# Hybrid SSD and attention block on one core: attention's product of probabilities and values as three float32r products

## The chip, the core and the metric

The kernel runs on one core of a Trainium2 chip. Its time is the device time of one execution in microseconds (us), the median of several runs. TensorE (PE) multiplies, VectorE (DVE) and ScalarE (ACT) do element-wise work, GpSimd (POOL) a little of it, and SyncE (SP) issues most transfers. Each engine works through its own list of instructions in order and waits on semaphores for the others.

## The reference, cut to what matters

One decoder block for 1024 tokens of width 1024. An SSD branch and a differential-attention branch read the same normed input; gates merge them, and a convolutional FFN follows. The attention branch, cut to its core:

```
q, k = partial_rope(...)                      # 16 half heads of 64
v = v.reshape(bsz, seq, 8, 128)               # 8 heads
for i in range(8):                            # query blocks of 128, causal
    s = einsum(q[block i], k[:q1]) * scale    # q1 = 128 * (i + 1)
    p = softmax(where(mask, s, -inf))
    attn = p[first of pair] - lam * p[second of pair]
    o[block i] = einsum(attn, v[:q1])
o = rms_norm(o, subln_w) * (1 - lam_init)
```

All is float32. The kernel reaches float32's accuracy in most of its matrix products with three float32r products, of a rounded high part and the remaining low part of each operand: high by high, high by low, low by high.

## The kernel before, in words

TensorE's lists of work are written out by hand (`manual_schedule` keeps the program's order on the engines that it names; in attention these are PE, DVE, ACT and POOL, while the order of SP's transfers there is the scheduler's). The stages are: the normed input with its first products; the projections of SSD and gates; the SSD stage, during which v is projected as filler; q and k and the output projection of SSD; attention, with the rest of q and k and the attention gate as filler; attention's output projection, the merge and `w_out`; the FFN's up and down products.

**v.** `v_stream` (L1018 on) makes v in 16 tiles of 128 tokens by 512 channels, each of 8 x 3 float32r products into a `wa` bank of PSUM (L1028 to L1030). ACT copies a tile into one half of the slot `vev`, and it is written to `vd` in memory as float32 (L1044). The generator is advanced by `fill(n)`, a few products at a time, between the SSD steps.

**Attention** goes over 64 items, 8 heads of 8 query blocks. For item t the list reads: `scores(t+1)`, in which the transposes of item t stand behind the score products (`behind`) and ahead of the mask and the maximum; `fill`; for i >= 4 the second half of the transposes; `probs(t+1)`, that is exponentials on ACT, then reciprocal, coefficient and the combination of both probabilities on DVE; `values(t)`; `fill`; the second half of values. A call of `fill` gives three products of 512 columns from `dense_stream`. 248 such calls are shared out over the items, and 20 are kept for each end.

`transposes(t, k0)` (L1496) turns up to four 128x128 blocks of the combined probabilities into the one `wb` bank (L1502), and ACT copies them to `aT` as float32 (L1503). `values` (L1508) multiplies each block with v's block of the same keys, one float32 product each (L1515), into a `wc` bank that gathers four query blocks. The mask is added at L1465 or L1475, the maximum taken at L1466 or L1476, the exponentials at L1478, L1486 and L1489, and the combination is L1492 to L1494. `load_heads` (L1426) fetches a head's v from `vd` into `vt`, two slots in turn, and `norm_o` and `out_o` norm and transpose the result.

`Slots` hands out 43 buffers of 4 KB per partition. `run_bg` and `later` keep a queue of small pieces for ACT and DVE, for instance the splits of the dense weights into high and low parts (L1381, L1384).

Of the kernel before, what the change touches and what calls it, by code (L numbers as in the profile page):

```python
# [11 lines left out]
F32 = mybir.dt.float32  # L12
F32R = mybir.dt.float32r
AF = mybir.ActivationFunctionType
ALU = mybir.AluOpType
AX = mybir.AxisListType

P = 128
D = 1024
S = 1024  # L20
HALF = 512
# [41 lines left out]
def kernel(ctx: ExitStack, tc: tile.TileContext, a: dict, out: bass.AP, dbg=None):  # L63
# [351 lines left out]
    sel = const("sel_r", [P, NH], F32R)  # L415

    zd = [dp.tile([P, D], F32, tag=f"zd{i}", name=f"zd{i}") for i in range(8)]
    vd = [dp.tile([P, D], F32, tag=f"vd{i}", name=f"vd{i}") for i in range(8)]
    yd = [dp.tile([P, D], F32, tag=f"yd{i}", name=f"yd{i}") for i in range(8)]
    gsd = [dp.tile([P, S], F32, tag=f"gsd{j}", name=f"gsd{j}") for j in range(8)]  # L420
    gad = [dp.tile([P, S], F32, tag=f"gad{j}", name=f"gad{j}") for j in range(8)]
# [533 lines left out]
    pairs_of_banks = ExitStack()  # L955
    pmm = pairs_of_banks.enter_context(tc.tile_pool(name="pmm2", bufs=1, space=bass.MemoryType.PSUM))
    BT, CT = [xbcT[8], xbcT[9]], [xbcT[10], xbcT[11]]
    vev = SL.get("vev", F32, (P, 2, HALF))

    SL.put(hi_t)  # L960

# [56 lines left out]
    def v_stream():  # L1018
        for vh in range(2):
            for i in range(8):  # L1020
                ps = ps_wa(f"v{vh}_{i}")
                half, q = divmod(i, 4)
                tsl = slice(q * P, (q + 1) * P)
                for k in range(KD):
                    need(("wv", vh, k // 2))
                    wh, wl = wv[vh, k // 2][0][:, k % 2, :], wv[vh, k // 2][1][:, k % 2, :]
                    xh_, xl_ = hT[k][half][:, 0, tsl], hT[k][half][:, 1, tsl]
                    T.matmul(ps, xh_, wh, start=(k == 0), stop=False)  # L1028
                    T.matmul(ps, xh_, wl, start=False, stop=False)  # L1029
                    T.matmul(ps, xl_, wh, start=False, stop=(k == KD - 1))  # L1030
                    if k % 2 == 0 and ((vh == 0 and i == 7 and k > 0) or (vh == 1 and i == 0 and k < 4)):
                        if v_low:
                            v_low.pop()()
                            if k == 4 and vh == 0:
                                v_raw.append(fetch_v(1, 3))
                        if v_raw:
                            v_low.append(split_v(1, (k // 2 - 1) % 4, v_raw.pop(0)))
                    if k < KD - 1:
                        yield
                if vh == 0 and i == 5:  # L1040
                    v_raw.extend(fetch_v(1, kp) for kp in range(3))
                e = vev[:, i % 2, :]
                A.copy(e, ps)
                SP.dma_start(vd[i][:, vh * HALF : (vh + 1) * HALF], e)  # L1044
                yield

    v_raw, v_low = [], []
# [202 lines left out]
            for r in range(2):  # L1250
                SP.dma_start(dst[64 * r : 64 * r + 64, :].bitcast(F32), src[m])

    SL.put(vev)
    yT = [[None] * 2 for _ in range(KD)]

    n_turn = 0
# [81 lines left out]
        SL.put(*yT[k])  # L1338


    vt = [SL.get(f"vt{i}", F32, (P, 8, P)) for i in range(2)]
    for t, n in ((qst, "qst"), (kst, "kst"), (klo, "klo")):
        t.append([SL.get(f"{n}1_{s}", F32R) for s in range(2)])
    thl = [[SL.get(f"tq{n}{i}", F32R) for n in ("hi", "lo")] for i in range(2)]
    pt_ = [[SL.get(f"p{b}_{s}") for s in range(2)] for b in range(2)]
    aTs = [SL.get(f"aT{i}", F32, (P, 2, 4, P)) for i in range(1)]
    osb = SL.get("osb", F32, (P, 2, 4, P))
    gev = SL.get("gev", F32, (P, 2, HALF))

    ssum = const("ssum", [P, 2, 2])  # L1350
    nmx = const("nmx", [P, 2, 2])
    rsm = const("rsm", [P, 2, 4, 2])
# [6 lines left out]
    blocks = [(kind, b) for b in (3, 4, 5) for kind in ("w_q", "w_k")] + [("ga", 0)]  # L1359
    blocks += [(kind, b) for b in (6, 7) for kind in ("w_q", "w_k")] + [("ga", g) for g in range(1, 8)]  # L1360
    emitted = {"scores": 0, "values": 0}
    raws, splits = {}, {}
    finished.clear()

# [32 lines left out]
    def dense_stream():  # L1397
        fetch(0)
        fetch(1)
        split_later(0)  # L1400
        for n, (kind, j) in enumerate(blocks):
            fetch(n + 2)
            need(("w", n))
            split_later(n + 1)
            w = splits.pop(n)
            for half in range(2):
                ps = ps_wa(f"{kind}p{j}_{half}")
                for k in range(KD):
                    xh_, xl_ = hT[k][half][:, 0, :], hT[k][half][:, 1, :]
                    T.matmul(ps, w[0][:, k, :], xh_, start=(k == 0), stop=False)  # L1410
                    T.matmul(ps, w[0][:, k, :], xl_, start=False, stop=False)
                    T.matmul(ps, w[1][:, k, :], xh_, start=False, stop=(k == KD - 1))
                    if k < KD - 1:
                        yield
                hsl = slice(half * HALF, (half + 1) * HALF)
                if kind == "ga":
                    A.activation(gev[:, half, :], ps, AF.Tanh, scale=0.5)
                    SP.dma_start(gad[j][:, hsl], gev[:, half, :])
                else:
                    hi, lo = thl[n % 2]  # L1420
                    A.activation(hi[:, hsl], ps, AF.Copy, scale=qscale[kind])
                    low_part(kind, j, half, ps, hi, lo)
                yield

    def load_heads(j):
        b = j % 2  # L1426
        last = 2 + ((j + 1) * 96 - 1) // P
        if last > 2:
            need(("low", "w_k", last, 1))
        assert emitted["scores"] >= 8 * (j - 1) and emitted["values"] >= 8 * (j - 1)  # L1430
        if j > 0:
            for s in range(2):
                load_qk(2 * j + s, qst[b][s], kst[b][s], klo[b][s])
        for kt in range(8):
            SP.dma_start(vt[b][:, kt, :], vd[kt][:, j * P : (j + 1) * P])

    stream = dense_stream()

# [57 lines left out]
    def transposes(t, k0):  # L1496
        j, i = items[t]
        nk = min(4, i + 1 - k0)
        ptr = ps_wb(f"at{j}_{i}_{k0}")
        at = aTs[0][:, (k0 // 4 + i) % 2]  # L1500
        for k in range(nk):
            T.transpose(ptr[:, k * P : (k + 1) * P], pt_[i % 2][0][:, (k0 + k) * P : (k0 + k + 1) * P], ident)  # L1502
        A.copy(at[:, :nk].rearrange("p k q -> p (k q)"), ptr[:, : nk * P])  # L1503
        return at, nk

    po_of = {}
# [1 line left out]
    def values(t, k0, at, nk):  # L1508
        j, i = items[t]
        grp, qi = divmod(i, 4)  # L1510
        if qi == 0 and k0 == 0:
            po_of[j, grp] = ps_wc(f"o{j}_{grp}").rearrange("p (q d) -> p q d", d=P)
        for k in range(nk):
            kt = k0 + k
            T.matmul(po_of[j, grp][:, qi, :], at[:, k, :], vt[j % 2][:, kt, :], start=(kt == 0), stop=(kt == i))  # L1515

    ob, oe = osb[:, 0], osb[:, 1].rearrange("p q d -> p (q d)")

# [73 lines left out]
    with tc.manual_schedule(engines={EN.PE, EN.DVE, EN.Activation, EN.Pool}):  # L1592
# [6 lines left out]
        for t, (j, i) in enumerate(items):  # L1599
            quota = (j * sum(share) + sum(share[: i + 1])) * nfill // (8 * sum(share)) - done  # L1600
            done += quota
            quota += 2 if t == len(items) - 2 else 0
            f1 = quota // 2
            nxt = t + 1 < len(items)
            x = {}

            def first_turn():
                x[0] = transposes(t, 0)

            if nxt:  # L1610
                sc = scores(t + 1, first_turn)
            else:
                first_turn()
            fill(f1)
            f2 = (quota - f1 + 1) // 2
            if i >= 4:
                x[4] = transposes(t, 4)
            if nxt:
                probs(t + 1, sc, 2)
            run_bg(1)  # L1620
            values(t, 0, *x[0])
            fill(f2)
            if i % 4 == 2 and pend is not None:
                out_o(*pend)
            if i >= 4:
                values(t, 4, *x[4])
            fill(quota - f1 - f2)
            run_bg(1)
            emitted["values"] += 1
            if t == 55:  # L1630
                SL.put(*thl[0], *thl[1], *qst[0], *kst[0], *klo[0], vt[0])
                stg = [SL.get(f"stg{i}", F32, (P, 2, HALF)) for i in range(2)]
                for _ in range(4):
                    att_in()
            elif t > 56:
                for _ in range(2 if i % 2 else 1):
                    if n_att < 10:
                        att_split()
            if j < 7 and i == (4 if j == 0 else 3):
                load_heads(j + 1)  # L1640
            if i % 4 == 3:
                norm_o(j, i // 4)
                pend = (j, i // 4)
            elif i % 4 == 2:
                pend = None
        SL.put(*pt_[0], *qst[1], *kst[1], *klo[1], *pt_[1], vt[1], *aTs)
        for n in range(NLAST - 2):
            if n == 11:
                out_o(*pend)
            if n == 1:  # L1650
                fetch_ao(0)
            fill(1)
            run_bg(1)
            if n % 2 == 1 and n < 9:
                att_split()
            if n == 13:
                split_ao(0)
        run_bg(len(bg))
        assert n_att == len(parts)
        SL.put(osb, gev, *stg)  # L1660
        for k in range(KD):
            SL.put(*hT[k])

# [757 lines left out]
```

## Time and profile before

| | |
|---|---|
| median of 3 runs | 1842.9 us (1842.53 to 1843.33) |
| profiled execution: span, first to last instruction | 5463.1 us |
| profiled execution: another time of its own | none is given beside the span |
| PE, PEld busy | 5447.4 us, 3303.6 us |
| DVE, ACT, POOL busy | 1312.2 us, 898.9 us, 139.0 us |
| DMA moved | 326.22 MB |
| granted TensorE clock in the records | 1.00 |

PE stands for products, PEld for loads of their stationary operand, which overlap products. The profiled execution took 2.96 times as long as the timed ones. Counts, order and shapes of its rows are those of the timed runs, and so is what an engine does; how far the durations on TensorE carry over is a matter for the prediction. In the trace, a float32 product stands as two records, a float32r product and a transpose as one.

### The profile page before, as it was taken

How to read it: one execution, taken by the hardware profiler on the slowest of the kernel's cores; microseconds unless marked ns; L12 is line 12 of the kernel's file. 1: busy time of each engine (PE TensorE's matmuls, PEld its weight loads, DVE VectorE, ACT ScalarE, POOL GpSimd, SP SyncE). 2: the span in 40 equal slices, each digit the busy share in tenths (PEclk: the TensorE clock that was granted, in tenths of full speed). 3: DMA queues.
4: the chain of work that ended last, by engine and by line, in shares of the span. 5: the costliest groups of instructions: out<-in, count | busy, mean ns of one | idle time of the engine just before them, and what ended most of it. 6: DMA issues, size and time to landing. Idle time of an engine off the chain costs nothing.

```text
span 5463.1 us, 24362 instructions
## 1 busy us (share of the span) xinstructions
PE 5447.4 (100%) x8922; PEld 3303.6 (60%) x8922; DVE 1312.2 (24%) x1984; ACT 898.9 (16%) x1744; POOL 139.0 (3%) x128
## 2 busy tenths in 40 slices
PE   9999999999999999999999999999999999999999
PEld 4555557766665555566677776556555555555555
DVE  4122222222221200022222231212333333332211
ACT  3111110011111100011122221102212111121210
POOL 0000000001110000000000000000000000000000
DMA  4021012212111212121122112210011111123221
GB/s 165 31 77 46 29 35 72 70 64 100 64 67 46 54 35 81 35 52 47 48 72 69 56 47 95 81 46 31 31 44 39 44 35 41 40 71 116 87 63 60
DMA packets 131368, 326.22 MB, mean 60 GB/s; under 512 B 14881, under 2 KB 39089, under 8 KB 131250
## 3 DMA queue, kind: packets, MB, share of 16 engines
q1 hardware_dynamic: 130290, 321.53, 18.2%
q0 software_dynamic: 960, 3.15, 0.2%
q8 instruction: 70, 1.15, 0.1%
q14 instruction: 48, 0.39, 0.0%
HBM read 229.45 MB, written 95.17 MB: 59 GB/s over the span
## 4 chain that ended last, share of the span: by engine, by line
PE 100%; issue 0%; ACT 0%; POOL 0%; DVE 0%; DMA 0%; DVEq 0%; POOLq 0%; ACTq 0%
PE upx L1822 4%; PE upx L1823 4%; PE upx L1821 4%; PE o L1515 4%; PE v L1028 2%; PE z L116 2%; PE v L1029 2%; PE z L118 2%; PE z L117 2%; PE xx L534 2%; PE so L117 2%; PE so L118 2%; PE xx L532 2%; PE upy L1821 2%; PE upy L1822 2%; PE upy L1823 2%
## 5 line engine op out<-in xcount | busy, mean ns | idle before, releaser
L1515 PEld LDWEIGHTS o<-vt,aT 128*128 128x128 f32 x576 | 201.1, 415 | 39.5 <-issue 33.8
L1821 PE MATMUL upx<-t,wu_t 128*128 128x512 f32 x264 | 218.9, 829 | 0.0
L1823 PE MATMUL upx<-t,wu_t 128*128 128x512 f32 x264 | 218.7, 828 | 0.0
L1822 PE MATMUL upx<-t,wu_t 128*128 128x512 f32 x264 | 218.7, 828 | 0.0
L1515 PE MATMUL o<-vt,aT 128*128 128x128 f32 x576 | 214.2, 578 | 0.0
L1456 PE MATMUL sc<-kst,qst 128*128 128x512 f32 (+2 forms) x192 | 141.7, 742 | 0.0
L1457 PE MATMUL sc<-klo,qst 128*128 128x512 f32 (+2 forms) x192 | 141.4, 746 | 0.0
L118 PE MATMUL so<-yT,w_ssd_o_lo 128*128 128x512 f32 x128 | 140.8, 1100 | 0.0
L117 PE MATMUL so<-yT,w_ssd_o_hi 128*128 128x512 f32 x128 | 140.8, 1100 | 0.0
L116 PE MATMUL so<-yT,w_ssd_o_hi 128*128 128x512 f32 x128 | 139.3, 1088 | 0.0
L1503 ACT COPY aT<-at 128x512 f32<-128x512 f32 (+2 forms) x96 | 45.9, 479 | 562.2 <-PE at L1502 562.2
L1822 PEld LDWEIGHTS upx<-t,wu_t 128*128 128x128 f32 x264 | 93.5, 354 | 63.8 <-issue 63.8
L1821 PEld LDWEIGHTS upx<-t,wu_t 128*128 128x128 f32 x264 | 93.4, 354 | 63.7 <-issue 62.7
L1823 PEld LDWEIGHTS upx<-t,wu_t 128*128 128x128 f32 x264 | 92.3, 350 | 63.8 <-issue 63.8
L1114 PEld LDWEIGHTS py<-xd,M 128*128 128x128 f32 x256 | 107.1, 596 | 34.8 <-issue 34.8
L1028 PE MATMUL v<-wv_hi,hT 128*128 128x512 f32 x96 | 121.5, 1266 | 0.0
L116 PE MATMUL z<-wz_hi,hT 128*128 128x346 f32 (+1 forms) x144 | 121.1, 841 | 0.0
L118 PE MATMUL z<-wz_hi,hT 128*128 128x346 f32 (+1 forms) x144 | 119.7, 832 | 0.0
L117 PE MATMUL z<-wz_lo,hT 128*128 128x346 f32 (+1 forms) x144 | 119.1, 827 | 0.0
L1502 PE MATMUL at<-ident,p 128*128 128x128 f32 x288 | 117.1, 576 | 0.0
L2184 PE MATMUL dx<-wdt_hi,g_hi 128*128 128x512 f32 x132 | 109.5, 830 | 0.0
L2186 PE MATMUL dx<-wdt_hi,g_lo 128*128 128x512 f32 x132 | 109.2, 827 | 0.0
(553 smaller groups left out, 10212.8 us busy)
## 6 DMA issues: line engine op xcount, KB each, us to landing
adas<-in_w_ada SPq DMA_DIRECT2D x32, 512.0 KB, 3.9
wdr<-in_w_down SPq DMA_DIRECT2D x22, 512.0 KB, 5.5
wtd<-wds SPq DMA_DIRECT2D x22, 512.0 KB, 2.9
wuf<-in_w_up SPq DMA_DIRECT2D x22, 512.0 KB, 3.5
gld_s<-gsum SPq DMA_DIRECT2D x22, 512.0 KB, 2.6
gst<-gld_s SPq DMA_DIRECT2D x20, 512.0 KB, 4.3
wdt_raw<-wtd SPq DMA_DIRECT2D x20, 512.0 KB, 3.9
wuv<-in_w_up SPq DMA_DIRECT2D x19, 512.0 KB, 3.6
```

The source lines that it names most:

```text
L116: T.matmul(ps, lh, rh, start=(i == 0), stop=False)
L117: T.matmul(ps, lh, rl, start=False, stop=False)
L118: T.matmul(ps, ll, rh, start=False, stop=(i == n - 1))
L1028: T.matmul(ps, xh_, wh, start=(k == 0), stop=False)
L1456: T.matmul(sc[:, n0:n1], qs_[s][:, tsl], ks_[s][:, n0:n1], start=True, stop=False)
L1457: T.matmul(sc[:, n0:n1], qs_[s][:, tsl], kl[s][:, n0:n1], start=False, stop=True)
L1502: T.transpose(ptr[:, k * P : (k + 1) * P], pt_[i % 2][0][:, (k0 + k) * P : (k0 + k + 1) * P], ident)
L1515: T.matmul(po_of[j, grp][:, qi, :], at[:, k, :], vt[j % 2][:, kt, :], start=(kt == 0), stop=(kt == i))
L1821: T.matmul(out_, wh, xh_, start=(k == 0 and first), stop=False, skip_group_check=not first)
L1822: T.matmul(out_, wh, xl_, start=False, stop=False, skip_group_check=not first)
L1823: T.matmul(out_, wl, xh_, start=False, stop=(k == end), skip_group_check=not first)
L2184: T.matmul(o, gh[:, kk, tsl], wh, start=(k == 0 and not more), stop=False, skip_group_check=more)
```

## The change

The product of probabilities and values is made of three float32r products for each 128x128 block, where it was one float32 product. For this v is split as it leaves its projection: ACT writes the high part and DVE subtracts it from PSUM for the low part, both go to one slot, and `vd` holds them beside each other, 128 high and 128 low channels for each head. `vt` has two slots per head instead of one. The transposed probabilities are split in the same way behind the transposes; `aT` has two slots instead of one. To find these slots the gate's buffer `gev` is left out until the 56th item; until then the gate is written through an idle buffer of the dense stream. Of the 14 splits of finished attention blocks two more move from the items to the tail behind them.

```diff
-    vd = [dp.tile([P, D], F32, tag=f"vd{i}", name=f"vd{i}") for i in range(8)]
+    vd = [dp.tile([P, 8, 2, P], F32, tag=f"vd{i}", name=f"vd{i}") for i in range(8)]
...
-    vev = SL.get("vev", F32, (P, 2, HALF))
+    vev = [SL.get("vev", F32R, (P, 4, 2, P))]
...
-                e = vev[:, i % 2, :]
-                A.copy(e, ps)
-                SP.dma_start(vd[i][:, vh * HALF : (vh + 1) * HALF], e)
+                e = vev[0]
+                v4 = lambda t: t.rearrange("p (j d) -> p j d", d=P)
+                A.activation(e[:, :, 0, :], v4(ps), AF.Copy)
+                V.tensor_tensor(e[:, :, 1, :], v4(ps), e[:, :, 0, :].bitcast(F32), op=ALU.subtract)
+                SP.dma_start(vd[i][:, 4 * vh : 4 * vh + 4], e.bitcast(F32))
...
-    vt = [SL.get(f"vt{i}", F32, (P, 8, P)) for i in range(2)]
+    vt = [[SL.get(f"vt{i}_{h}", F32R, (P, 4, 2, P)) for h in range(2)] for i in range(2)]
...
-    aTs = [SL.get(f"aT{i}", F32, (P, 2, 4, P)) for i in range(1)]
+    aTs = [SL.get(f"aT{i}", F32R, (P, 2, 4, P)) for i in range(2)]
     osb = SL.get("osb", F32, (P, 2, 4, P))
-    gev = SL.get("gev", F32, (P, 2, HALF))
...
                 if kind == "ga":
-                    A.activation(gev[:, half, :], ps, AF.Tanh, scale=0.5)
-                    SP.dma_start(gad[j][:, hsl], gev[:, half, :])
+                    e = gev[half] if gev else thl[n % 2][0].bitcast(F32)[:, hsl]
+                    A.activation(e, ps, AF.Tanh, scale=0.5)
+                    SP.dma_start(gad[j][:, hsl], e)
...
-            SP.dma_start(vt[b][:, kt, :], vd[kt][:, j * P : (j + 1) * P])
+            SP.dma_start(vt[b][kt // 4][:, kt % 4].bitcast(F32), vd[kt][:, j])
...
-        at = aTs[0][:, (k0 // 4 + i) % 2]
+        at = aTs[(k0 // 4 + i) % 2]
...
-        A.copy(at[:, :nk].rearrange("p k q -> p (k q)"), ptr[:, : nk * P])
+        hi, lo = [at[:, n, :nk].rearrange("p k q -> p (k q)") for n in range(2)]
+        A.copy(hi, ptr[:, : nk * P])
+        V.tensor_tensor(lo, ptr[:, : nk * P], hi.bitcast(F32), op=ALU.subtract)
...
-            T.matmul(po_of[j, grp][:, qi, :], at[:, k, :], vt[j % 2][:, kt, :], start=(kt == 0), stop=(kt == i))
+            o = po_of[j, grp][:, qi, :]
+            vh, vl = [vt[j % 2][kt // 4][:, kt % 4, n, :] for n in range(2)]
+            T.matmul(o, at[:, 0, k, :], vh, start=(kt == 0), stop=False)
+            T.matmul(o, at[:, 0, k, :], vl, start=False, stop=False)
+            T.matmul(o, at[:, 1, k, :], vh, start=False, stop=(kt == i))
...
+                gev_t = SL.get("gev", F32, (P, 2, HALF))
+                gev += [gev_t[:, h, :] for h in range(2)]
...
-                    if n_att < 10:
+                    if n_att < 8:
                         att_split()
...
-            if n % 2 == 1 and n < 9:
+            if n % 2 == 1 and n < 13:
                 att_split()
```

More of the change, by code (lines that the diff above doesn't have):

```diff
@@ L1251, in load_qk @@
                 SP.dma_start(dst[64 * r : 64 * r + 64, :].bitcast(F32), src[m])
-    SL.put(vev)
+    SL.put(*vev)
     yT = [[None] * 2 for _ in range(KD)]
@@ L1361 @@
     emitted = {"scores": 0, "values": 0}
+    gev = []
     raws, splits = {}, {}
@@ L1630 @@
             if t == 55:
-                SL.put(*thl[0], *thl[1], *qst[0], *kst[0], *klo[0], vt[0])
+                SL.put(*thl[0], *thl[1], *qst[0], *kst[0], *klo[0], *vt[0])
+                gev_t = SL.get("gev", F32, (P, 2, HALF))
+                gev += [gev_t[:, h, :] for h in range(2)]
                 stg = [SL.get(f"stg{i}", F32, (P, 2, HALF)) for i in range(2)]
@@ L1645 @@
                 pend = None
-        SL.put(*pt_[0], *qst[1], *kst[1], *klo[1], *pt_[1], vt[1], *aTs)
+        SL.put(*pt_[0], *qst[1], *kst[1], *klo[1], *pt_[1], *vt[1], *aTs)
         for n in range(NLAST - 2):
@@ L1659 @@
         assert n_att == len(parts)
-        SL.put(osb, gev, *stg)
+        SL.put(osb, gev_t, *stg)
         for k in range(KD):
```

## The prediction

> **What bounds the kernel now.** I read the page first: its span, the busy times, and the shares of the chain that ended last.
>
> ```profile
> span 5463.1 us, 24362 instructions
> PE 5447.4 (100%) x8922; PEld 3303.6 (60%) x8922; DVE 1312.2 (24%) x1984; ACT 898.9 (16%) x1744; POOL 139.0 (3%) x128
> PE 100%; issue 0%; ACT 0%; POOL 0%; DVE 0%; DMA 0%; DVEq 0%; POOLq 0%; ACTq 0%
> ```
>
> TensorE is never idle, but the span is 2.96 times the median of 1842.9 us: the profiled execution ran TensorE far slower than the timed ones. I therefore read TensorE's rows as counts and the other engines' rows as times. The second view is the chain that ended last, in order of time (start, length, what): an attention item early, two places later on, and one before attention.
>
> ```profile
> 2424.36 0.84 PE w_qp L1410
> 2426.88 0.21 PE sc L1456
> 2427.09 0.21 PE sc L1457
> 2427.30 0.30 PE sc L1456
> 2427.60 0.42 PE sc L1457
> 2428.02 1.63 PE at L1502 x4
> ...
> 2441.94 3.36 PE o L1515 x8
> ...
> 2680.46 0.84 PE gap L1411
> 2681.30 0.62 PE gap L1412
> ...
> 3110.12 2.35 PE o L1515 x8
> ```
>
> ```profile
> 1312.66 2.83 PE pb L1092 x8
> 1315.49 1.01 PE v L1028
> ```
>
> Everything fits one unit, a slot. Until 2681 us a float32r product of 512 columns takes 0.84 us and a float32 record of 128 columns 3.36/8 = 0.42 us: two slots and one. From 2681 us on a slot is 2.35/8 = 0.294 us. A float32 product makes two records (576 in L1515 for 8 x 36 = 288 key blocks), so it costs two slots. The float32r products of 128 columns are L1092 and the short scores: after a long product the first two take 0.21 us, half a slot, and then they settle at 0.42. Eight of L1092 take 2.83 us and delay the next product by 1.01 - 0.84 = 0.17: 3.00 us, 7.1 slots. So a short float32r product costs a whole slot as soon as it stands in a row, since PE's weight load then sets the pace, and a row saves about 0.9 slot behind a long product.
>
> The trace holds 2681/0.42 + (5463 - 2681)/0.294 = 15,846 slots. The median gives at most 1842.9/15,846 = 0.116 us each. At full speed PE can't be busy throughout:
>
> ```profile
> 0.00:100.00 100.00, 90.22 (x106) 43.14 (x107) 57.96 (x107) 47.58 (x88) 3.98 (x8) 1.00 0.59 226
> 1100.00:1750.00 650.00, 650.00 (x1016) 411.83 (x1016) 142.66 (x210) 99.63 (x261) 84.03 (x64) 1.00 0.20 71
> 2300.00:3350.00 1050.00, 1050.00 (x2138) 718.31 (x2138) 261.32 (x523) 224.11 (x586) 16.49 (x16) 1.00 0.21 60
> ```
>
> (Window, its length, busy PE, weight load, DVE, ACT, POOL; start, SSD stage, attention.) In the first 100 us DVE works 58 us against 100/0.42 = 238 slots, 28 us at that price, so some 30 us are start-up: (1842.9 - 30)/15,846 = 0.114. I take 0.115 us a slot. In attention, 381/0.42 + 669/0.294 = 3183 slots are 366 us at full speed, against 261 us of DVE: DVE, 25% busy in the profile, is really about 70% busy.
>
> **The change part by part.** Value products: 288 blocks at three short float32r products instead of two float32 records. Upper bound: a slot more each, 288 x 0.115 = +33 us. Of the 96 rows, 64 follow a long dense product and save up to 0.9 slot, so at least 230 x 0.115 = +26 us. I take 33, since rows behind transposes save nothing, and carry 26 as the bound.
> The Trainium skill (TensorE: Matmul & The Clock Gate, section LDWEIGHTS (loading the stationary operand)) puts the load of 128 columns at 128/1.2 = 107 ns, whatever is multiplied by them. By that figure, as an estimate, this term would be +31 us; the trace agrees that short products go at the pace of their loads (a slot each in L1092), and shows no full-speed time.
>
> The low part of aT: 96 new DVE subtractions from PSUM. Their place matters more than their sum. In DVE's list of the built kernel each item's first one stands directly ahead of the next item's mask and maximum, and it waits for the four transposes and for ACT's copy (now the high part). Queued behind it: mask, maximum, exponentials, the combination, and so the next item's transposes, at which PE stops in order. Before, the mask could start with the scores' end. The rows of attention, by form:
>
> ```profile
> L1476 DVE TENSOR_REDUCE nmx<-sc 128x1 f32<-128x1024 f32 x16 | 19.6, 1225 | 0.6
> L1475 DVE TENSOR_TENSOR sc<-sc,maskneg 128x128 f32<-128x128 f32 x64 | 19.2, 300 | 220.9 <-PE sc L1457 220.9
> L1476 DVE TENSOR_REDUCE nmx<-sc 128x1 f32<-128x640 f32 x16 | 13.2, 825 | 0.5
> L1493 DVE SCALAR_TENSOR_TENSOR coef<-ssum,nlam,rsm 128x1 f32<-128x1 f32 x62 | 13.6, 220 | 2.2
> L1465 DVE TENSOR_TENSOR sc<-sc,maskneg 128x256 f32<-128x256 f32 x30 | 13.0, 432 | 200.3 <-PE sc L1457 200.3
> L1494 DVE SCALAR_TENSOR_TENSOR p<-p,coef,p 128x1024 f32<-128x1024 f32 x8 | 10.3, 1285 | 0.3
> L1492 DVE RECIPROCAL rsm<-ssum 128x2 f32<-128x2 f32 x62 | 10.2, 165 | 195.2 <-ACT p L1486 132.4 <-ACT p L1489 62.5
> L1494 DVE SCALAR_TENSOR_TENSOR p<-p,coef,p 128x512 f32<-128x512 f32 x8 | 6.0, 752 | 0.3
> L1391 DVE SCALAR_TENSOR_TENSOR tqlo<-w_kp,tqhi 128x512 fp32r<-128x512 f32 x10 | 6.9, 692 | 50.0 <-ACT tqhi L1421 50.0
> ```
>
> ```profile
> L1503 ACT COPY aT<-at 128x512 f32<-128x512 f32 x48 | 28.1, 585 | 350.8 <-PE at L1502 350.8
> L1489 ACT ACTIVATE p<-sc,nmx 128x512 f32<-128x512 f32 x16 | 10.8, 683 | 1.2 <-DVE nmx L1466 1.2
> L1486 ACT ACTIVATE p<-sc,nmx 128x1024 f32<-128x1024 f32 x8 | 9.0, 1119 | 0.0
> L1486 ACT ACTIVATION_READ_ACCUMULATOR p<-sc,nmx 128x1 f32 x32 | 6.5, 204 | 0.0
> L1503 ACT COPY aT<-at 128x128 f32<-128x128 f32 x15 | 4.0, 265 | 40.2 <-PE at L1502 40.2
> ```
>
> Widths between are taken on the straight line through two rows of an operation. The low part does the work of L1391 (692 ns at 512 columns) and, narrow, of L1475 (300 at 128).
>
> For query block n two times compete. The turn is PE's work from the end of scores(n) to the end of scores(n+1), in slots: n transposes and 2n of values for the block before, 24 of dense work (8 x 31 calls of three long products; 18 in one of eight turns), and the scores. The chain is mask, maximum, exponentials, reciprocal, coefficient, combination. For n = 7: turn 7 + 24 + 14 + 4 = 49 slots = 5.64 us; chain 2 x 0.300 + 2 x 1.225 + 1.119 + 0.204 + 0.165 + 0.220 + 1.285 = 6.04, less half the scores (8 slots, 0.92), as the first head's mask starts early: 5.12. The turn wins. For n = 1 to 7 and then 0 (whose block before is 7, so 8 + 24 + 16 + 4 slots) I get turns of 3.80, 4.37, 5.17, 4.83, 6.10, 6.67, 5.64, 5.98 and chains of 3.32, 3.94, 4.56, 3.82, 4.33, 4.73, 5.12, 2.70. So the longer is the turn each time, 42.6 us a head, 340 us for 8 heads.
>
> After: each turn has a slot more per block of values, and the chain first pays transposes, copy and low part: 4 x 0.115 + 0.585 + 0.692 = 1.74 us from n = 4 on, and 0.68, 1.03, 1.38 for n = 1, 2, 3; from n = 4 on it loses the early start as well. Turns 3.91, 4.60, 5.52, 5.29, 6.67, 7.36, 6.44, 6.90; chains 4.00, 4.97, 5.94, 6.25, 6.76, 7.27, 7.78, 4.44. The longer ones sum to 50.0 us a head, 400 us: +59. In it stands a hand-over that the sum lacks, PE to ACT behind the transposes. The timeline has it:
>
> ```profile
> 3106.87 1.39 PE L1502 MATMUL at<-ident,p 128*128 128x128 f32 x4
> 3107.88 1.00 PE L1410 MATMUL gap<-b,ga_hi 128*128 128x512 f32 x1
> 3108.35 0.59 ACT L1503 COPY aT<-at 128x512 f32<-128x512 f32 x1 [5.26 <-PE at L1502]
> ```
>
> The copy starts 0.47 us after PE took up its next work, at the slowed clock; between 0 and 0.47 I take 0.25. On every chain that makes +73 us for attention (59 to 85), the 33 us of slots within it. If dense work's splits or the squares of the norm sit in the chain, too, no turn covers anything, and the whole delay counts: 119 us.
>
> The split of v: 16 low parts of 0.69 us on DVE, and each waits for ACT's copy. In the SSD stage DVE has 143 us against 650/0.42 = 1548 slots = 178 us, so cover exists on average: 0 to 11 us, and I take +5. The single vev buffer must land before the next tile is copied out; a tile of v is 24 long products, 48 slots, 5.5 us even with nothing between: hidden.
> vd and vt move twice the bytes with as many DMAs: 8.4 MB more on 326, and a head's v is loaded four items ahead, over 20 us: nothing. The gate's buffer and the two high-low splits moved into the tail stand under the 18 calls of dense work at the end: nothing; uncovered, each would cost about an ACT and a DVE pass of 512 columns, like L1503 and L1391, 1.3 us.
>
> Sum: 1842.9 + 73 + 5 = 1921 us. A measurement of this kernel can tell about 0.2% from no change.
>
> **The rivals.** (a) Only the slots count, because the chain stays covered: 1842.9 + 26 to 33, about 1873. For it: all turns of before are longer than the chains, by 0.4 us at the least. Against: the delay is 0.7 to 1.7 us.
> (b) No cover at all: 119 and 11, about 1970. For it: DVE is in order and splits of the dense weights and norms run on it between items; against: most of them stand where DVE waits for exponentials.
> (c) Faster: three passes instead of four. If the weight loads ran ahead in the values as for the first two rows of L1456 and L1457 (0.21 us, half a slot), 288 x (1.5 - 2) x 0.115 = -17 us and 1826; it decides if the load of the next weights hides behind half a slot and the chain stays covered. Against it: the following short ones at 0.42, and L1092's 7.1 slots for eight. The Trainium skill (FP8 and Floating Point Precision, TensorE Precision Notes) counts a true float32 product as four passes, and by that rule three reduced ones would gain; the trace speaks against it.
> (d) Gains and losses cancel: loads half ahead, -5 to +5 us.
>
> **How the numbers follow.** Forecast 0.60; (a) 0.20; (b) 0.13; (c) 0.04; (d) 0.03. From 1866 (under (a)'s 1842.9 + 26) to 1965 (most of the way to (b)) all of forecast and (a) is held and a part of (b), so less than 2 in 10 is out. Faster 0.04, same 0.03, slower 0.93.
>
> **What would show it.** In the profile after: 864 records in L1521 to L1523 that take a slot each in the chain (12 in a row about 11 slots, 0.42 or 0.294 us each); 96 new DVE rows of about 0.55 us ahead of each mask; the mask starting behind them. PE's slowed clock hides the longer chain in a profile, so if only 288 slots are added there while the time grows by far more than 33 us, step two is right; a growth of 26 to 33 makes it wrong. Short products at 0.21 us all along would make the first step wrong.

## The result and the profile after

The changed kernel takes 1927.6 us (1925.9 to 1930.1, 4 runs), the kernel before 1843.1 us: a ratio of 1.0459, 95% interval 1.0444 to 1.0474, 84 us slower. The profiled execution of the changed kernel has a span of 1927.2 us and a time of 1929.1 us, so 1.9 us lie around the span, and this profile was taken at full speed.

The page of the changed kernel: span, busy times, the chain that ended last.

```profile
span 1927.2 us, 25080 instructions
PE 1876.4 (97%) x9210; PEld 1555.0 (81%) x9210; DVE 1361.4 (71%) x2096; ACT 895.1 (46%) x1744; POOL 142.7 (7%) x128
PE 70%; DVE 14%; ACT 6%; DMA 3%; issue 3%; SPq 1%; POOL 1%; ACTq 0%; DVEq 0%; POOLq 0%
```

Here DVE and ACT carry a fifth of the chain. The slow profile of before has all of it on PE, but that is the wrong one to compare with: in the full-speed profile of before, in the first experiment below, DVE and ACT carry 9%. There are 288 more products, and 112 more DVE rows (96 for the probabilities, 16 for v).

The same stretch of attention in the chain in order of time (start, length, what; the longest pieces), first of the changed kernel:

```profile
801.07 0.45 PE at L1504 x4
801.54 0.59 ACT aT L1506
802.16 0.69 DVE aT L1507
802.85 0.22 DVE sc L1477
803.09 1.10 DVE nmx L1478
804.22 1.10 ACT p L1480 x2
805.32 0.27 ACT aT L1506
805.63 0.33 PE o L1521
806.09 0.33 PE o L1523
```

and of the kernel before, from the full-speed profile of the first experiment below:

```profile
801.97 0.46 PE at L1502 x4
802.43 0.23 PE w_qp L1410
802.66 0.23 PE w_qp L1411
802.89 0.24 PE w_qp L1412
803.13 0.04 issue
803.16 1.16 PE o L1515 x8
804.32 0.23 PE w_qp L1410
```

Before, the chain stays on PE from the transposes through dense work into the values. After, it leaves PE behind the transposes: copy, low part, mask, maximum, exponential, and then the second copy, which stands behind that exponential in ACT's list and for which the values wait. The slots are as forecast: a dense product 0.23 us, four transposes 0.46.

The view of a line's instructions with their first and last start gives the length of the stages. The last product of `dense_stream` in its forms for attention, before and after (first q block, last gate block), and the last product of v's projection, before and after:

```profile
L1412 PE MATMUL w_qp<-hT,w_q_lo x60: 389/393/398, 643.1 to 851.7; 128*128 128x512 f32 x60
L1412 PE MATMUL gap<-hT,ga_lo x96: 389/393/400, 761.9 to 1021.8; 128*128 128x512 f32 x96
L1030 PE MATMUL v<-wv_hi,hT x96: 388/395/401, 336.8 to 504.1; 128*128 128x512 f32 x96
```

```profile
L1413 PE MATMUL w_qp<-hT,w_q_lo x60: 389/393/398, 649.8 to 901.6; 128*128 128x512 f32 x60
L1413 PE MATMUL gap<-hT,ga_lo x96: 388/393/400, 791.3 to 1108.2; 128*128 128x512 f32 x96
L1030 PE MATMUL v<-wv_hi,hT x96: 388/395/400, 337.0 to 510.8; 128*128 128x512 f32 x96
```

Attention: 1021.8 - 643.1 = 378.7 us before, 1108.2 - 649.8 = 458.4 after, +79.7. The stage with v's projection: 167.3 and 173.8, +6.5. Together 86.2 of the 86.7 us between the two spans; the rest of the kernel is unchanged. In this profile of the changed kernel the recorded clock is 0.50 for 6.8 us of attention (the last section shows it), so up to 3.4 of the 79.7 us, an estimate, are the clock's and not the change's.

### The profile page after: what moved, and what is told of

It is laid out like the page before. It is cut to its first block, busy times and chain, and to the rows that moved or that the text cites. A ratio compares the mean times of both kernels' runs of the same rounds, so it can differ in the third digit from the quotient of the medians.

```text
span 1927.2 us, 25080 instructions
## 1 busy us (share of the span) xinstructions
PE 1876.4 (97%) x9210; PEld 1555.0 (81%) x9210; DVE 1361.4 (71%) x2096; ACT 895.1 (46%) x1744; POOL 142.7 (7%) x128
## 4 chain that ended last, share of the span: by engine, by line
PE 70%; DVE 14%; ACT 6%; DMA 3%; issue 3%; SPq 1%; POOL 1%; ACTq 0%; DVEq 0%; POOLq 0%
PE upx L1832 4%; PE upx L1833 4%; PE upx L1831 4%; DVE nmx L1478 2%; DVE aT L1507 2%; PE upy L1832 2%; PE upy L1831 2%; PE at L1504 2%; PE upy L1833 2%; PE dx L2195 2%; PE dx L2196 2%; PE dx L2194 2%; ACT aT L1506 2%; PE z L117 2%; PE z L118 2%
## 5 line engine op out<-in xcount | busy, mean ns | idle before, releaser
L1507 DVE TENSOR_TENSOR aT<-at,aT 128x512 fp32r<-128x512 f32 (+2 forms) x96 | 53.5, 558 | 87.5 <-ACT aT L1506 86.4
L1831 PE MATMUL upx<-t,wu_t 128*128 128x512 f32 x264 | 103.1, 391 | 0.5 <-DVE cv L2259 0.4
L1832 PE MATMUL upx<-t,wu_t 128*128 128x512 f32 x264 | 102.8, 390 | 0.2 <-DVE t L1949 0.2
L1833 PE MATMUL upx<-t,wu_t 128*128 128x512 f32 x264 | 102.7, 389 | 0.0
L1521 PE MATMUL o<-vt,aT 128*128 128x128 f32 x288 | 80.5, 279 | 4.8 <-ACT aT L1506 4.1
L95 DVE TENSOR_TENSOR g_lo<-gst,g_hi 128x1024 fp32r<-128x1024 f32 (+1 forms) x42 | 47.6, 1135 | 50.6 <-ACT g_hi L94 50.4
L1522 PE MATMUL o<-vt,aT 128*128 128x128 f32 x288 | 79.5, 276 | 0.0
L1521 PEld LDWEIGHTS o<-vt,aT 128*128 128x128 f32 x288 | 55.8, 194 | 16.5 <-ACT aT L1506 15.2
L1478 DVE TENSOR_REDUCE nmx<-sc 128x1 f32<-128x640 f32 (+3 forms) x64 | 65.6, 1025 | 2.2
L1458 PE MATMUL sc<-kst,qst 128*128 128x512 f32 (+2 forms) x192 | 64.3, 342 | 0.0
L1459 PE MATMUL sc<-klo,qst 128*128 128x512 f32 (+2 forms) x192 | 63.3, 346 | 0.0
L1849 DVE SCALAR_TENSOR_TENSOR ug<-cg,vec,ug 128x1023 f32<-128x1023 f32 (+1 forms) x44 | 56.3, 1280 | 6.1 <-ACT ug L1848 5.3
L1504 PE MATMUL at<-ident,p 128*128 128x128 f32 x288 | 50.5, 285 | 10.0 <-DVE p L1496 8.9
L1523 PEld LDWEIGHTS o<-vt,aT 128*128 128x128 f32 x288 | 55.6, 193 | 5.3 <-DVE aT L1507 5.0
L1831 PEld LDWEIGHTS upx<-t,wu_t 128*128 128x128 f32 x264 | 49.5, 188 | 11.8 <-DVE cv L2259 1.3
L1504 PEld LDWEIGHTS at<-ident,p 128*128 128x128 f32 x288 | 32.1, 141 | 33.1 <-DVE aT L1507 13.8
L1832 PEld LDWEIGHTS upx<-t,wu_t 128*128 128x128 f32 x264 | 49.6, 188 | 10.6 <-DVE t L1949 0.5
```

What stands on the lines that cost most here:

```text
L1458: T.matmul(sc[:, n0:n1], qs_[s][:, tsl], ks_[s][:, n0:n1], start=True, stop=False)
L1459: T.matmul(sc[:, n0:n1], qs_[s][:, tsl], kl[s][:, n0:n1], start=False, stop=True)
L1478: V.reduce_max(nmx[:, bq, s : s + 1], sc[:, :L], axis=AX.X, negate=True)
L1507: V.tensor_tensor(lo, ptr[:, : nk * P], hi.bitcast(F32), op=ALU.subtract)
L1521: T.matmul(o, at[:, 0, k, :], vh, start=(kt == 0), stop=False)
L1522: T.matmul(o, at[:, 0, k, :], vl, start=False, stop=False)
```

## The experiments

**The kernel before, profiled again.** No edit.

> The kernel before once more, for a profile of it. If its profile is taken at full speed, the theory (products cost a slot of about 0.114 us as long as they stand in a row, and before the change PE's turn covers the chain in attention) expects 0.227 us for a product of 512 columns, about 0.114 us for a float32 record of 128, and an attention stage in which PE seldom waits for DVE: a stage of about 375 us, some 80 us shorter than after the change. The rival (only the slots count) expects a stage 33 us shorter and PE waiting for DVE there as often as after. Time 1843 us.

1842.6 us, span 1840.5 us, and this profile runs at full speed. Its page:

```profile
span 1840.5 us, 24362 instructions
PE 1816.6 (99%) x8922; PEld 1520.9 (83%) x8922; DVE 1300.1 (71%) x1984; ACT 892.4 (48%) x1744; POOL 141.4 (8%) x128
PE 86%; DVE 6%; ACT 3%; DMA 1%; issue 1%; POOL 0%; SPq 0%; DVEq 0%; POOLq 0%; ACTq 0%
```

The long product takes 0.227 us and attention 378.7 us, as the theory expected. In attention PE waits for DVE 2.6 us in all, against 19.7 us in the changed kernel (8.9 for the combination, 8.5 and 2.3 for the low part). The 8 float32 records above take 1.16 us in the chain, because their first weight load had to wait for ACT's copy and starts with them; other rows of 8 take 0.89 us.

Slots read from the slowed profile carry over, but not what it shows of short products behind a long one. The row of eight on L1092 that the prediction reads, now at full speed:

```profile
337.89 0.84 PE pb L1092 x8
338.73 0.28 PE v L1028
```

The row and the delay of the next long product are 0.84 + 0.28 - 0.23 = 0.89 us, 7.8 slots of 0.1135 us, where the slowed profile had 7.1. The saving of 0.9 slot a row is 0.2 at full speed.

DVE's busy time is the same in both profiles (1312 and 1300 us), so there it is indeed 71% of the real span.

**No low part of the probabilities, PE's work unchanged.**

```diff
-        V.tensor_tensor(lo, ptr[:, : nk * P], hi.bitcast(F32), op=ALU.subtract)
...
-            T.matmul(o, at[:, 1, k, :], vh, start=False, stop=(kt == i))
+            T.matmul(o, at[:, 0, k, :], vl, start=False, stop=(kt == i))
```

> The changed kernel without the low part of the transposed probabilities: no subtraction on DVE ahead of the mask, and the third product of a block takes the high part and v's low part once more in its place, so the low part's share of the result is left out. TensorE's work is the same. Theory (the longer chain is over half of the loss): the table's turns then win everywhere, and 40 to 45 us come back, 1885 us. Rival (only the slots count): no change, 1928 us.

1878.4 us (ratio to before 1.0195, 1.0178 to 1.0212): 49.2 us come back from 96 subtractions of 0.56 us, 53 us of busy time on an engine that is idle for 29% of the span. The rival is out. This run takes away both the place of the subtraction and its hold on the `wb` bank; the moved low part below separates them in part.

**The low part alone, on the kernel before.** (Two splits move to the tail as in the change, since a buffer is taken.)

```diff
-        A.copy(at[:, :nk].rearrange("p k q -> p (k q)"), ptr[:, : nk * P])
+        hi = at[:, :nk].rearrange("p k q -> p (k q)")
+        A.copy(hi, ptr[:, : nk * P])
+        V.tensor_tensor(scr[:, : nk * P], ptr[:, : nk * P], hi, op=ALU.subtract)
```

> The kernel before with one thing added: DVE subtracts the copied transposes from PSUM at the place that the change gives the low part, into a scratch buffer that nobody reads. Products stay float32, v is not split. Theory: the longer chain alone, the table with two slots a block, 405 against 336 us: about 65 us slower than before, 1908 us. Rival (only the slots count): DVE has room, so under 10 us slower, 1843 to 1853 us.

1907.7 us (ratio 1.0352, 1.0337 to 1.0368): 64.8 us from a result that nobody reads. Alone it costs 16 us more than on top of the third product, since added slots on PE hide a part of the chain, as the longer of turn and chain says. The waits of PE's weight loads in attention (who waited for whom: us, times, longest) name the places; the longest rows of each kernel follow. This kernel:

```profile
PEld o L1518 <- ACT aT L1505: 22.3, 24, 1.6
PEld at L1503 <- issue: 18.1, 24, 1.3
PEld ot L1545 <- DVE scr L1506: 15.6, 8, 2.4
PEld at L1503 <- DVE scr L1506: 14.3, 31, 0.5
```

The changed kernel:

```profile
PEld o L1521 <- ACT aT L1506: 15.2, 24, 1.2
PEld at L1504 <- issue: 13.6, 25, 1.1
PEld at L1504 <- DVE aT L1507: 13.4, 29, 0.5
PEld ot L1550 <- DVE aT L1507: 11.9, 8, 2.0
PEld o L1523 <- DVE aT L1507: 5.0, 17, 0.4
```

The kernel before:

```profile
PEld o L1515 <- ACT aT L1503: 4.6, 10, 0.6
PEld at L1502 <- PE sc L1457: 2.0, 3, 0.9
```

The same four places in both kernels with a low part: values that wait for a copy on ACT, transposes without a named releaser (read here as loads for transposes that wait for the combination, since PE's own waits in the changed kernel have "PE at L1504 <- DVE p L1496", 8.9 us, 25 times as well), and transposes of the second half and of the output (`ot`) that wait for DVE to leave the one `wb` bank.

**v without its low part.** The low half is zero.

```diff
+    G.memset(vev[0].bitcast(F32), 0.0)
...
-                V.tensor_tensor(e[:, :, 1, :], v4(ps), e[:, :, 0, :].bitcast(F32), op=ALU.subtract)
```

> The changed kernel without the low part of v at the projection: ACT's high part and the doubled writes stay, DVE's 16 subtractions are left out and the low half of the buffer is zero. My estimate of this term was +5 us (0 to 11), so 1917 to 1928 us, most likely 1923. A rival in which the SSD stage carries much of the loss expects 1900 us or less.

1924.2 us (1921.5 to 1926.4): 3.4 us less than the changed kernel, on the expected side; the two kernels' runs touch, so the sign of it rests on the stage. There the last v product starts 168.3 us behind the first, against 173.8 and 167.3:

```profile
L1031 PE MATMUL v<-wv_hi,hT x96: 388/395/401, 337.5 to 505.8; 128*128 128x512 f32 x96
```

So the 16 subtractions are worth 5 to 5.5 us there, and the doubled writes and the single buffer about 1 us. (The profiles of three other runs with the split and without a record of half clock in this stage have 173.2 to 173.4 us; the low part alone, without the split, has 167.3 again.)

**The low part behind the maximum.**

```diff
-        V.tensor_tensor(lo, ptr[:, : nk * P], hi.bitcast(F32), op=ALU.subtract)
+        low = lambda: V.tensor_tensor(lo, ptr[:, : nk * P], hi.bitcast(F32), op=ALU.subtract)
+        if k0 == 0 and t + 1 < len(items):
+            late.append(low)
+        else:
+            low()
...
             V.reduce_max(nmx[:, bq, s : s + 1], sc[:, :L], axis=AX.X, negate=True)
+            if s == 1 or i > 4:
+                low_late()
```

> The changed kernel with the first low part of an item moved in DVE's list: behind the next item's maximum (for query blocks 5 to 7 behind the first of their two maxima) instead of ahead of the mask. Nothing else changes: same products, same subtractions. Theory (the place ahead of the mask is what costs): the subtraction then runs while ACT makes exponentials, the chain is covered again, and the time falls to that of the kernel without low parts, 1878 to 1885 us. Rival (96 subtractions cost wherever they stand, since DVE has too much to do in attention, or the single bank of the transposes is held longer and PE waits for it instead): 1910 us or more.

1904.3 us (ratio 1.0331, 1.0314 to 1.0348): between the two expectations. The place ahead of the mask is worth 23 us of the 49. The other 26 us, by the list of waits, became these two rows of 30 us:

```profile
PEld o L1536 <- DVE aT L1516: 15.3, 25, 1.3
PEld at L1513 <- DVE aT L1516: 14.9, 32, 0.8
```

The waits for the copy and those without a name are nearly gone (a row of 3.7 us is left for the copy); now the third product waits for the late low part, and the second half's transposes still wait for the bank. No run gave the transposes a second bank, so what that wait costs by itself stays open.

**Value products slipped in among long ones.** As the kernel with the low part behind the maximum, and up to two short products stand behind each long one; the products with the low part come last in an item.

```diff
+    def slip(n=2):
+        for _ in range(min(n, len(shorts))):
+            shorts.popleft()()
...
                     T.matmul(ps, w[0][:, k, :], xh_, start=(k == 0), stop=False)
+                    slip()
```

> As the one with the low part behind the maximum, and the value products are not issued in a row: up to two stand behind each long product of 512 columns (dense work and scores). Theory (a short float32r product costs a slot only because its weight load sets the pace in a row; behind a long product the load is hidden and it costs half a slot, 0.057 us): 864 products, 80 to 90% of them slipped in, 40 to 44 us less than with the low part behind the maximum, about 1838 us, near or under the 1843 us of the kernel before. Rival (a short product costs a slot anywhere, or only one load can run ahead): no gain, or half of it, 1860 to 1885 us.

1886.1 us (ratio 1.0235, 1.022 to 1.025): 18 us less than with the products in a row, under half of what the theory asked for, and, as the next run shows, hardly for its reason. The wait of the values for the low part is gone from the list, because the third products come later; that of the transposes for the bank stays (15.6 us). The next run takes the low part out to see slipping alone.

**Slipped, without a low part.** As above with `low = lambda: None`, the third product as in the second experiment.

> Three short products a block without low parts of the probabilities (the third takes the high part and v's low part again), and up to two of them behind each long product instead of in a row. No engine but TensorE has anything to win or lose by it. Theory now (a weight load can run under one product only, the one ahead of it, so a short product costs a slot wherever it stands): the same as with the products in a row, 1875 to 1881 us. Rival, and my view before the run with slipped products (loads hide behind long products, half a slot each): 35 to 45 us less, about 1838 us.

1875.6 us (1874.3 to 1876.8), against 1878.4 (1877.1 to 1879.6) in a row: within 3 us, no half slots. So of the 18 us at most 3 are slots, and the other 15 are, by the lists of waits, the 15.3 us for which values waited for the late low part. The chain in order of time shows why:

```profile
801.10 0.28 PE gap L1421
801.38 0.17 PE o L1546 x2
801.56 0.28 PE w_qp L1417
801.84 0.17 PE o L1546 x2
802.01 0.28 PE w_qp L1419
```

One long product and two short ones take 801.56 - 801.10 = 0.46 us, two slots and two slots. The first short one starts its successor after half a slot, and the next long one gives it back. Both runs fit one reading: the load of the next weights runs under one product only, the one ahead of it, takes a slot, and does not fit under a short one.

**Two products a block, no low part.**

```diff
-            T.matmul(o, at[:, 0, k, :], vl, start=False, stop=False)
-            T.matmul(o, at[:, 1, k, :], vh, start=False, stop=(kt == i))
+            T.matmul(o, at[:, 0, k, :], vl, start=False, stop=(kt == i))
```

> The kernel without low parts of the probabilities, and with only two short products a block, high by high and high by v's low part: the third product and the low part's share of the result are left out. Theory (a short float32r product costs one slot of 0.1135 us, a float32 product of the same shape two): 288 slots less than with three, 33 us, so 1846 us; that is the kernel before plus what the split of v costs. Rival (a short product costs half a slot or a little over in a long row): 16 to 20 us less, about 1860 us.

1849.5 us (ratio 1.0037, 1.0024 to 1.0050), 28.9 us less than with three. Attention is back at its length before, 1027.0 - 648.4 = 378.6 us against 378.7:

```profile
L1413 PE MATMUL w_qp<-hT,w_q_lo x60: 389/393/398, 648.4 to 857.0; 128*128 128x512 f32 x60
L1413 PE MATMUL gap<-hT,ga_lo x96: 389/393/403, 767.2 to 1027.0; 128*128 128x512 f32 x96
L1030 PE MATMUL v<-wv_hi,hT x96: 388/397/516, 336.5 to 509.5; 128*128 128x512 f32 x96
```

Two short float32r products cost what one float32 product costs. The 6.6 us left over the 1842.9 of before are those of the split of v: the stage with its projection takes 173.0 us against 167.3. The other parts of the change (the gate's buffer, two splits moved to the tail) show no cost.

## Why the prediction was right

The forecast was 1921 us, measured 1927.6, and the runs take the loss apart in the forecast's own terms: v split +6.6 (1842.9 to 1849.5), third product +28.9 (to 1878.4), low part +49.2 (to 1927.6).

**Slots.** Forecast 26 to 33, taken 33; measured 28.9, 0.100 us for each of 288 products against a price of 0.115. The price itself was right: a long product, two slots, takes 0.227 us at full speed. The Trainium skill (TensorE: Matmul & The Clock Gate, section LDWEIGHTS (loading the stationary operand)) gives a load of 128 columns 128/1.2 = 107 ns; in rows, short products here start 0.11 us apart. The missing 4 us are about what PE's loads wait less in attention with three products than with two (5.7 us in all where it is 10.3, the kernels without low parts); that reading was not tested by itself. Two of a block's three products have the same stationary operand, the high part, and the trace has a load for each of them all the same (288 on each of L1521 and L1522); whether one load can serve both was not tried.

**The low part.** Forecast 73 - 33 = 40 us, measured 49.2. The cause is shown from both sides: taken away it gives back 49, alone on the kernel before it costs 65 where the table with two slots a block asked for 65 to 69. So the comparison of turn and chain held. Its picture of where PE stops did not: I had PE stop at the next item's transposes alone. It stops at them, at the second half's values, because ACT's second copy stands behind the delayed exponential, and at the transposes of second halves and of the output, because DVE now holds the one `wb` bank longer. I had named copy and low part as queued ahead of the mask, but not who waits for the bank; that wait is in the changed kernel 13.4 + 11.9 us of the loads' waits, and the size of this term came out near because the stops add up to the same longer chain.

The traces show this turn by turn. Measured from the start of an item's last score product to that of the next item's (medians over the heads), the turns sum to 43.4 us a head before and 53.2 after, where the table with the hand-over of 0.25 us has 42.6 and 51.6. The table has the long chain of block 7 stop PE behind the next head's first scores, so that, measured this way, the turn of n = 7 would grow by 0.97 us and that of n = 0 by 2.51. They grew by 2.34 and 1.14: PE stops a turn earlier, at the transposes of the output, which wait 11.9 us in 8 heads for DVE to leave the bank, and the sum is the same 3.48 us.

**The split of v.** Forecast +5 (0 to 11), measured 6.6, of which 5 to 5.5 us are the subtractions. The writes and the single buffer, which the forecast put at nothing, are the other 1 us or so.

**The rivals.** Slots alone (1873) fell with the second and third experiments. No cover at all (1970) was too much. Faster by half slots fell with the slipped products: the two products at 0.21 us that spoke for it are half a slot in their start, and whoever follows pays it back. My own statement that a row saves 0.9 slot behind a long product holds in the slowed profile alone (0.2 slot at full speed), so that the lower bound of 26, which I made of it, was near the measured 28.9 by luck. No change at all, (d), fell with the measurement.

No version ran under the kernel before: with three products for two float32 records, 29 us are lost before anything waits, and the best of them that computes the whole result stays at 1886 us. Even with two products and the low part left out it is 1849.5 us.

## What to carry to other kernels

Count TensorE work in slots, the larger of the columns streamed and the load of the next weights, as these runs read: with 128 columns a float32r product is no cheaper than half a float32 product, so three of them lose to one, in a row or behind long ones. Before a subtraction is given to an engine with 30% to spare, look at what stands behind it in that engine's list and which buffer it keeps: here 53 us of DVE work cost 49 us at 71% load. Moving such an operation needs all of its waits moved, or a part of the time reappears at the next one: here 26 of the 49 us.

## What the runs showed of the hardware beyond that

One profile of the kernel before had TensorE at 0.42 and then 0.294 us a slot, another of the same kernel at 0.114; the timed runs agree with the second. A long product was two slots at all three speeds, and the busy times of DVE and ACT differ by under 1%.

What slowed TensorE stays open. The slow profile holds no record of the clock (its page has no row PEclk, where the others have one), so the 1.00 that its views print, and that the table of before repeats, is no measurement. Where there is a record, the slot follows it. The changed kernel's profile has one of 0.50 over 6.8 us of attention (a window, with the clock in the third place from the end, and two pieces of the chain in it):

```profile
923.00:929.80 6.80, 6.80 (x27) 6.32 (x28) 3.53 (x7) 1.70 (x4) 0.00 (x0) 0.50 0.62 198
924.40 0.21 PE o L1523
926.43 0.43 PE w_kp L1412
```

A short product takes 0.21 us there and a long one 0.43, against 0.11 and 0.23 at full clock. The 0.42 us of the slow profile is twice that again.
